# Last head of the forgetting attention: row maxima issued over another stretch, two gate projections moved, buffers re-placed

## The chip, the cores and the metric

The kernel runs on one core of a Trainium2 chip. The core has a matrix engine (PE, with its weight loads listed apart as PEld), a vector engine (DVE), a scalar engine (ACT), a general engine (POOL) and a queue engine (SP) that only starts transfers. Each engine works through its own list of instructions in order and waits at semaphores for the others. The metric is the device time of one execution in microseconds (us), lower is better.

## What is computed

One decoder layer on a sequence of 2048 rows with 1024 columns. The input is normalised and projected; eight heads of forgetting attention (branch A) and eight heads of windowed attention (branch B) work on the projections; each branch's output is multiplied by a gate, both go through one output projection, which is normalised and added to the input. Cut to what matters:

```python
h = rms_norm(x, g_pre[l]) * (1.0 + scale[:, None, :]) + shift[:, None, :]
proj = h @ w_in[l]
qa, ka, va, fa, za, qb, kb, vb, zb = jnp.split(proj, split_points, axis=-1)
oa = forgetting_attention(qa, ka, va, fa + b_fgate[l])   # 8 heads of 64, causal
oa = oa * jax.nn.silu(za)
ob = sliding_window_sink_attention(qb, kb, vb, sinks[l]) # after rope
ob = ob * jax.nn.silu(zb)
y = jnp.concatenate([oa, ob], axis=-1) @ w_out[l]
x = x + gate[:, None, :] * rms_norm(y, g_post[l])
# in forgetting_attention, per block of 128 queries:
s = q @ k.T * d**-0.5 + cum[query] - cum[key]; s = where(causal, s, -inf)
p = softmax(s); out = p @ v
```

## The kernel before

All matrix products are made from pairs of 16-bit numbers (a high and a low part), three matmuls for one product. The kernel has four stages: the start and branch B (to about 454 us of the trace), the heads of branch A (454 to 1017 us), and the output projection, whose first part lies inside the last head of branch A and whose rest runs to the end.

**Heads and steps.** Branch A is 8 heads of 20 steps, 160 steps `s` in all, with `hd, r = divmod(s, 20)`; step 7.3 below means head 7, step 3 (s = 143). A step is one column group of 512 queries (`ci` 0 to 3, in steps 0-1, 2-5, 6-11, 12-19 of a head) against two blocks of 128 keys. Its width `w` is 1024 columns, less in the two steps on the diagonal (896 and 384). A step does: `exp32` (ACT, L1312, from the score tile `sta` to `p`), `high` (ACT, L1320) and, a step later, `low` (DVE, L1323), which split `p` in two 16-bit parts `pha`; the scores of the next step (PE, L1307 and L1308, four matmuls); and the products with the values of the step two back (`pv`, PE, L1333 to L1336). There is one score tile, so the scores of step s+1 wait for `exp32` of step s.

**Work put between.** Two lists are spread over the steps, and they go on PE between `pv` and the next scores:

- `punits`: projection units, each 3 matmuls of 512 columns (L328); 8 units fill one bank, which is then read by ACT and DVE. From step 0.0 on there are 352 of them: for each head 1 to 7 four column groups of query and key (`qk`, written to the tile `T` of that head by `evac_qk`), and for each head 0 to 7 two gate groups (`za`, through `evac_z`: tanh on ACT L378, product on DVE L368, store to `z_d` by POOL L376). A loop near L1057 writes their order: for a head `qk` 0, 1, 2, `za`, `qk` 3, `za`, where the `za` belong to the head before.
- `munits`: the row maxima of the scores (`max_units`): a matmul of up to 512 columns (PE, L1258), then a maximum along the row (DVE, L1261, or L1263 with the mask), and after the last of a group a short chain on DVE (L1270 to L1278) and a small matmul (`ext_rows`, L1216) whose result goes into `T` by a transfer (L1222). They must be done before the head's scores of that group, and run most of a head ahead; 44 of them belong to one head.

How many of each go into a step is set by two running goals. Units: the share of the width `w` done so far, of the width of heads 0 to 6, times 352, plus 14, but no more than 352. Maxima: 26 plus 44/20 for each step, to the end of the list. The two are interleaved, half of them before the next scores and half behind the `pv`.

**The last head.** In step 7.0 `open_out` releases the normalised input h^T (`hT`, four tiles of 16 KB per partition) and puts the output weights `wohl` and buffers there. The 16 pieces of w_out are loaded by SP (L1393) into six buffers of `stpo`, and split by ACT and DVE (`w_out_split`, L1398 and L1399) from step 7.2 on. In steps 7.4 and 7.6 `Out.load` fetches the first two output tiles (the attention output `o_d`, L1413, and the gate `z_d`, L1415), and in 7.6 and 7.8 `Out.turn` transposes them on PE (L1421), multiplies by the gate on DVE (L1430), takes squares on ACT (L1434, into a junk tile), sums them on PE (L1438) and writes the high part on ACT (L1444) and the low part on DVE (L1445), each some ticks after the other. Two ticks make a step. Products of the output projection (`Out.product`, PE L1458) come from step 7.10 on; the rest follows after the last step. The x rows and the y rows of a tile lie in the pool `oxy`.

Of the kernel before, what the change touches and what calls it, by code (L numbers as in the profile page):

```python
# [10 lines left out]
F32 = mybir.dt.float32  # L11
F16 = mybir.dt.float16
# [28 lines left out]
def hybrid_layer(  # L41
# [72 lines left out]


    right = ExitStack()
    hpx = ExitStack()
    hpool = hpx.enter_context(tc.tile_pool(name="hpool", bufs=1))
    wpool = right.enter_context(tc.tile_pool(name="wpool", bufs=2, side="right"))
# [9 lines left out]
    swx = ExitStack()  # L129
    swc = swx.enter_context(tc.tile_pool(name="swc", bufs=1))  # L130

    hT = [hpool.tile([P, 2, KT, CH], F16, name=f"hT{i}") for i in range(NCH)]
# [54 lines left out]
    def after(n, f):  # L187
        late.append([n, f])
# [173 lines left out]

    def evac_z(kt, key, ci):
        def evac(ps, free):
            t = op_.tile([P, CH], F32, tag="tz", name="tz")

            def mul():
                V.scalar_tensor_tensor(t[:], t[:], 1.0, ps, op0=ALU.add, op1=ALU.mult)  # L368
                free()
                if lag[0]:  # L370
                    after(lag[0], store)
                else:
                    store()

            def store():
                G.dma_start(z_d[kt, :, ci * CH:(ci + 1) * CH], t[:])  # L376

            after(1, lambda: A.activation(t[:], ps, AF.Tanh, scale=czs[key][:]))  # L378
            after(2, mul)

        return evac


    xt, rstd, xlate = {}, {}, {}

    def load_x(t):
        if t // 4 == 1:
# [668 lines left out]
    N_V3 = len(punits)  # L1056
    for hd in range(1, 9):  # L1057
        for part in range(6):
            if part in (3, 5):
                add(f"za{(hd - 1) // 2}", za_units(hd - 1, (part - 3) // 2))  # L1060
            elif hd < 8:
                add(f"qk{hd}", qk_units(hd, (0, 1, 2, 0, 3)[part]))
    windows = [Pair(j, i) for j in range(4) for i in range(0, NB, 2)]
    pos = [0]

# [293 lines left out]
            munits += us[:2] + ([ext] if ext else []) + us[2:]  # L1359
            ext = ext2  # L1360
    munits += [lambda: None, lambda: None, ext]
    M_HEAD, M_LEAD, PV_LAG = 44, 26, 2

# [3 lines left out]
    def w_slot(n):  # L1367
        return oio["w"][:, n // KT, n % KT, :]

    def open_out():  # L1370
        nonlocal op_, stp
        foxl.close()
        hpx.close()
        wo = foxo.enter_context(tc.tile_pool(name="wo", bufs=1, reuse_waits="tile"))
        op_ = foxo.enter_context(tc.tile_pool(name="opo", bufs=2, reuse_waits="tile"))
        stp = foxo.enter_context(tc.tile_pool(name="stpo", bufs=6, reuse_waits="tile"))
        oxy = foxo.enter_context(tc.tile_pool(name="oxy", bufs=2, reuse_waits="tile"))
        oio["x"] = lambda: oxy.tile([P, D], F32, tag="xr", name="xr")
        oio["y"] = lambda: oxy.tile([P, D], F32, tag="yg", name="yg")
# [9 lines left out]

    def w_out_load(m):  # L1390
        k, cc = m % KT, slice((m // KT) * CH, (m // KT + 1) * CH)
        w_raw[m] = stp.tile([P, CH], F32, tag="st", name=f"wo{m}")
        SP.dma_start(w_raw[m][:], w_out0[k * P:(k + 1) * P, cc])  # L1393

    def w_out_split(m):
        k, cc = m % KT, slice((m // KT) * CH, (m // KT + 1) * CH)
        raw, hi = w_raw.pop(m), w_slot(k)[:, cc]
        A.activation(hi, raw[:], AF.Copy, scale=wsc[:, k:k + 1])  # L1398
        V.scalar_tensor_tensor(w_slot(8 + k)[:, cc], raw[:], wsc[:, k:k + 1], hi, op0=ALU.mult, op1=ALU.subtract)  # L1399

    oio = {}

    class Out:

# [12 lines left out]
        def turn(self, lag):  # L1417

            px = [bk[bank()][:].rearrange("p (k n) -> p k n", k=4) for _ in range(2)]
            for k in range(KT):  # L1420
                PE.transpose(px[k // 4][:, k % 4, :], self.o[:, k * P:(k + 1) * P], ident[:])  # L1421
            self.hl = wpool.tile([P, 2, KT, P], F16, tag=("whl", "wraw")[self.t % 2], name="oz")
            self.sc = sm(1, "w_pw")
            hi, lo = self.hl[:, 0], self.hl[:, 1]
            gs = sm(1, "w_mx")

            def gate():
                for h in range(2):
                    z = self.z[:, 4 * h:4 * h + 4, :]
                    V.tensor_tensor(z, px[h], z, op=ALU.mult)  # L1430

            def squares_():
                junk = stp.tile([P, KT, P], BF16, tag="st", name="zj")
                A.activation(junk[:], self.z, AF.Square, accum_out=gs[:])  # L1434
# [9 lines left out]
            after(lag + 1, lambda: A.activation(hi, self.z, AF.Copy, scale=self.sc[:]))  # L1444
            after(lag + 2, lambda: V.scalar_tensor_tensor(lo, self.z, self.sc[:], hi, op0=ALU.mult, op1=ALU.subtract))  # L1445

        def product(self, n, k):
            cc = slice(n * CH, (n + 1) * CH)
            if k == 0:
                self.b = bank(True)  # L1450
                if n == 0:
                    self.ss = sm(2, "y_ss")
                else:
                    self.x = oio["x"]()
                    SP.dma_start(self.x[:], xs[self.t * P:(self.t + 1) * P, :])
            py, b = bk[self.b][:], self.b
            for m_, (i, j) in enumerate(((0, 0), (0, 1), (1, 0))):
                PE.matmul(py, self.hl[:, i, k, :], w_slot(8 * j + k)[:, cc],  # L1458
                          start=(k == 0 and m_ == 0), stop=(k == KT - 1 and m_ == 2))
            if k < KT - 1:  # L1460
                return

            def evac():
                if n == 0:
                    self.y = oio["y"]()
                junk = stp.tile([P, 2, CH], BF16, tag="st", name="yj")
                A.activation(junk[:, 0, :], py, AF.Square, accum_out=self.ss[:, n:n + 1])
# [52 lines left out]
    with tc.manual_schedule():  # L1520
# [18 lines left out]
        for _ in range(3):  # L1539
            tick()  # L1540
        steps[0].scores()
        p0, p_tot = pos[0], len(punits) - pos[0]

        w_at = {2: [0], 3: [1], 4: [2], 5: [3], 6: [4], 8: [5], 10: [6], 11: [7], 12: [8], 13: [9], 14: [10],
                15: [11, 12], 16: [13, 14], 17: [15]}
# [109 lines left out]
```

## Time and profile before

| what | value |
|---|---|
| median of 3 runs | 1188.02 us (1186.71 to 1188.46) |
| the profiled execution's own time | 1186.6 us |
| its span, first to last instruction | 1184.9 us |
| mean granted TensorE clock | 0.988 |
| instructions | 27012 |
| step 0.0 begins (first `exp32`) | 453.6 us |
| `exp32` of step 6.7 / 6.16 / 7.0 begins | 902.7 / 933.9 / 943.7 us |
| `exp32` of step 7.4 / 7.10 begins | 953.4 / 976.5 us |

A row of the windows view gives, for a stretch of the span, the busy time of each engine with its number of instructions, the granted TensorE clock as a share of full speed, and the load of the transfer engines. A row of the waits view names an instruction and the one that ended its wait, with the sum, the number of times and the longest. A row of the timeline view has the start, the duration and the instruction. In a timeline, a matmul's duration overlaps the next one, so the time that one takes from PE is the distance between two starts.

### The profile page before, as it was taken

To read this page: it belongs to the slowest core of one execution; us is meant where nothing else is said; L and a number is where in the kernel's file an instruction comes from. 1 tells how busy PE (TensorE), PEld (TensorE's weight loads), DVE (VectorE), ACT (ScalarE), POOL (GpSimd) and SP (SyncE) were. 2 spreads that over 40 slices of the span, in tenths; PEclk is the share of its full clock that TensorE was granted. 3 is DMA by queue.
4 is the path that set the end of the run, shared out by engine and by line. 5 is a ranking of instruction groups with operands and counts; after the bars stand their busy time and mean duration, and the time that the engine had idled before them with its cause. 6 is when DMAs were issued, how large, how long until landed. Compare 5 with 4: busy or idle time off the path is not lost. (4 is left out here: it accounts for less than half of the span.)

```text
span 1184.9 us, 27012 instructions
## 1 busy us (share of the span) xinstructions
PE 1122.8 (95%) x10490; PEld 655.1 (55%) x10490; DVE 919.1 (78%) x2329; ACT 677.6 (57%) x1122; POOL 165.9 (14%) x302
## 2 busy tenths in 40 slices
PE   5899998999989999999999999999999979999996
PEld 1466556644459855555555555555555545555553
DVE  6776577888787657889888897888878897767665
ACT  4676445565456434666766666666766788333331
POOL 1001122233232201211111111011000100000000
PEclk9999999999999999999999999999999989999999
DMA  9645336587667722333323323133121154465652
GB/s 331 213 137 158 94 88 123 113 150 143 141 132 119 130 63 70 78 93 78 85 68 103 75 61 86 45 90 64 40 48 46 59 156 156 147 191 168 210 172 78
DMA packets 162452, 136.36 MB, mean 115 GB/s; under 512 B 95356, under 2 KB 139428, under 8 KB 162324
## 3 DMA queue, kind: packets, MB, share of 16 engines
q1 hardware_dynamic: 152532, 106.65, 35.8%
q0 software_dynamic: 9456, 27.72, 8.9%
q8 instruction: 82, 1.34, 0.5%
q14 instruction: 46, 0.38, 0.1%
q10 hardware_dynamic: 336, 0.26, 0.1%
HBM read 70.97 MB, written 25.18 MB: 81 GB/s over the span
## 5 line engine op out<-in xcount | busy, mean ns | idle before, releaser
L1312 ACT ACTIVATE p<-sta,lift,scl_qk 128x1024 f32<-128x1024 f32 (+2 forms) x160 | 171.7, 1073 | 99.2 <-PE sta L1308 90.7
L328 PE MATMUL bk<-hT,wh_qk 128*128 128x512 f16 x768 | 194.6, 378 | 0.0
L1458 PE MATMUL bk<-wohl,oz 128*128 128x512 f16 x768 | 172.4, 379 | 1.9 <-ACT wohl L1398 0.8
L1323 DVE TENSOR_TENSOR pha<-p,pha 128x1024 f16<-128x1024 f32 (+2 forms) x160 | 169.3, 1058 | 0.2 <-ACT pha L1320 0.2
L1320 ACT ACTIVATE pha<-p 128x1024 f16<-128x1024 f32 (+2 forms) x160 | 148.1, 926 | 35.0 <-POOL p L1316 29.6
L1261 DVE TENSOR_REDUCE a_m<-bk 128x1 f32<-128x512 f32 x192 | 129.8, 684 | 43.6 <-PE bk L1258 43.1
L1458 PEld LDWEIGHTS <-oz 128*128 128x128 f16 x768 | 74.4, 99 | 83.9 <-issue 1.8
L1307 PE MATMUL sta<-T 128*128 128x512 f16 (+1 forms) x320 | 110.7, 351 | 10.5 <-ACT p L1312 10.5
L1333 PE MATMUL poa<-vt,pha 128*128 128x65 f16 x1088 | 117.6, 194 | 2.3 <-DVE ona L1342 2.3
L1336 PE MATMUL poa<-vt,pha 128*128 128x65 f16 x1088 | 117.2, 193 | 1.4 <-DVE pha L1323 1.4
L1335 PE MATMUL poa<-vt,pha 128*128 128x64 f16 x1088 | 117.5, 195 | 0.0
L328 PEld LDWEIGHTS <-wh_qk 128*128 128x128 f16 x768 | 72.4, 97 | 74.7 <-issue 0.6
L1333 PEld LDWEIGHTS <-pha 128*128 128x128 f16 x1088 | 102.4, 97 | 16.8 <-DVE ona L1342 3.2
L1258 PE MATMUL bk<-T 66*128 66x512 f16 (+2 forms) x320 | 109.9, 350 | 1.0 <-DVE a_m L1261 1.0
L1308 PE MATMUL sta<-T 69*128 69x512 f16 (+1 forms) x320 | 109.3, 352 | 0.0
L1335 PEld LDWEIGHTS <-pha 128*128 128x128 f16 x1088 | 101.7, 98 | 13.6 <-issue 0.3
L1336 PEld LDWEIGHTS <-pha 128*128 128x128 f16 x1088 | 101.5, 99 | 1.6 <-DVE pha L1323 1.6
L328 PE MATMUL bk<-hT,wh_za 128*128 128x512 f16 x384 | 99.8, 378 | 0.0
L346 PE MATMUL bk<-wh_va,hT 128*128 128x128 f16 x1536 | 94.3, 221 | 1.7 <-DVE wh_va L272 1.7
L328 PE MATMUL bk<-hT,wh_zb 128*128 128x512 f16 x384 | 92.7, 384 | 2.2 <-DVE wh_zb L272 2.2
L346 PEld LDWEIGHTS <-hT 128*128 128x128 f16 x1536 | 89.0, 99 | 8.3 <-issue 5.9
L1316 POOL TENSOR_SCALAR_AFFINE_SELECT p<-p 128x256 f32<-128x256 f32 x64 | 33.0, 515 | 420.6 <-ACT p L1312 417.9
(487 smaller groups left out, 1860.5 us busy)
## 6 DMA issues: line engine op xcount, KB each, us to landing
wa<-in_w_ada_dram SPq DMA_DIRECT2D x16, 512.0 KB
z_d<-tz POOLq DMA_DIRECT2D x32, 256.0 KB, 3.0
T<-stq SPq DMA_DIRECT2D x128, 64.0 KB
T<-o_d SPq DMA_DIRECT2D x16, 512.0 KB
T<-z_d SPq DMA_DIRECT2D x16, 512.0 KB
xr<-in_x_dram SPq DMA_DIRECT2D x16, 512.0 KB
out_dram<-yg SPq DMA_DIRECT2D x15, 512.0 KB
xt<-in_x_dram SPq DMA_DIRECT2D x12, 512.0 KB
```

The costliest lines, as they stand in the source:

```text
L328: PE.matmul(ps, whl[:, a, k, :], hT[ci][:, b, k, :], start=(k == 0 and n == 0), stop=(k == KT - 1 and n == 2))
L346: PE.matmul(ps[:, u * P:(u + 1) * P], hT[ci][:, a, k, u * P:(u + 1) * P], whl[:, b, k, :], start=(k == 0 and n == 0), stop=(k == KT - 1 an ...
L1258: PE.matmul(mx[:, :w], T[0:XM, 0, i * P:(i + 1) * P], T[0:XM, 2, pc * CH:pc * CH + w], start=True, stop=True)
L1261: V.tensor_reduce(m3[:, u, pc:pc + 1], mx[:, :w], axis=AX.X, op=ALU.max)
L1307: PE.matmul(self.st[:, o:o + w], T[:, 3, kb_], T[:, 1, qc], start=True, stop=False)
L1312: A.activation(self.p32[:, :self.w], self.st[:, :self.w], AF.Exp, scale=scl[f"qk{self.hd}"][:], bias=lift[:])
L1320: A.activation(self.ph[:, 0, :self.w], self.p32[:, :self.w], AF.Copy)
L1323: V.tensor_tensor(self.ph[:, 1, :self.w], self.p32[:, :self.w], self.ph[:, 0, :self.w], op=ALU.subtract)
L1333: PE.matmul(po[:, u, :], ph[:, 0, pq], vt[:, b, hd, 0:65], start=(self.first and n == 0 and u == 0), stop=False)
L1335: PE.matmul(po[:, u, 0:64], ph[:, 0, pq], vt[:, b, hd, 65:VW], start=False, stop=False)
L1336: PE.matmul(po[:, u, :], ph[:, 1, pq], vt[:, b, hd, 0:65], start=False, stop=(self.last and n == len(self.blocks) - 1))
L1458: PE.matmul(py, self.hl[:, i, k, :], w_slot(8 * j + k)[:, cc], start=(k == 0 and m_ == 0), stop=(k == KT - 1 and m_ == 2))
```

## The change

1. **Row maxima.** From step 6.7 on (`m_from` = 127) the goal of the maxima is a line from where they stand to the end of the list, reached with step 7.3 (`m_done` = 143). Before, the list ended with step 7.8.
2. **Projection units.** `P_LAST` = 16 units, the two gate groups of head 7, are held back and issued in steps 7.0 to 7.7, two a step. The others are spread over heads 0 to 6 with 14 ahead, as 322 units for their whole width (before 352, with the cap at the end). By the two goals, units issued in steps 0.0 to 6.6 go from 331 to 304, in 6.7 to 6.15 from 21 to 23, in 6.16 to 6.19 from 0 to 9, in 7.0 to 7.7 from 0 to 16. Maxima go, in the same stretches, from 279 to 279, 20 to 25, 9 to 12, and 18 to 12, and two in step 7.8 to none.
3. **Order.** For head 7, `qk` 3 comes before both `za`.
4. **Places.** The gate units of head 7 read `hT` 2 and 3, so these two tiles now stay (pool `hpb`). The x and y rows of the output tiles lie in `hT[3]`, the w_out pieces from the sixth on and the junk of the squares in `hT[2]`, the last gates in the freed `gw`. `stpo` has 4 buffers in place of 6.

The core of the diff:

```diff
+    hpb = ctx.enter_context(tc.tile_pool(name="hpb", bufs=1))
...
+    hT = [(hpool if i < 2 else hpb).tile([P, 2, KT, CH], F16, name=f"hT{i}") for i in range(NCH)]
...
-            t = op_.tile([P, CH], F32, tag="tz", name="tz")
+            t = oio["z"][ci % 2] if "w" in oio else op_.tile([P, CH], F32, tag="tz", name="tz")[:]
...
-            if part in (3, 5):
-                add(f"za{(hd - 1) // 2}", za_units(hd - 1, (part - 3) // 2))
+            if part in ((4, 5) if hd == 7 else (3, 5)):
+                add(f"za{(hd - 1) // 2}", za_units(hd - 1, part // 5))
             elif hd < 8:
-                add(f"qk{hd}", qk_units(hd, (0, 1, 2, 0, 3)[part]))
+                add(f"qk{hd}", qk_units(hd, ((0, 1, 2, 3) if hd == 7 else (0, 1, 2, 0, 3))[part]))
...
-    M_HEAD, M_LEAD, PV_LAG = 44, 26, 2
+    M_HEAD, M_LEAD, PV_LAG, P_LEAD, P_LAST = 44, 26, 2, 14, 16
...
-        stp = foxo.enter_context(tc.tile_pool(name="stpo", bufs=6, reuse_waits="tile"))
-        oxy = foxo.enter_context(tc.tile_pool(name="oxy", bufs=2, reuse_waits="tile"))
+        stp = foxo.enter_context(tc.tile_pool(name="stpo", bufs=4, reuse_waits="tile"))
+        oxy = [hT[3][:, a, 4 * b:4 * b + 4, :].rearrange("p k n -> p (k n)").bitcast(F32)
+               for a in range(2) for b in range(2)]
...
+        gz = gat.tile([P, D], F32, tag="gw", name="gz")
+        oio["z"] = [gz[:, n * CH:(n + 1) * CH] for n in range(2)]
+        spare = hT[2][:].rearrange("p a k n -> p (a k n)")
+        oio["r"] = [spare[:, 2 * CH * n:2 * CH * (n + 1)].bitcast(F32) for n in range(6)]
+        oio["j"] = [spare[:, CH * a:CH * b].bitcast(BF16) for a, b in ((12, 14), (14, 15), (15, 16))]
...
-        w_raw[m] = stp.tile([P, CH], F32, tag="st", name=f"wo{m}")
+        w_raw[m] = oio["r"][(m - 5) % 6] if m > 4 else stp.tile([P, CH], F32, tag="st", name=f"wo{m}")[:]
...
-        p0, p_tot = pos[0], len(punits) - pos[0]
+        p0, p_tot = pos[0], len(punits) - pos[0] - P_LEAD - P_LAST
+        m_ramp, m_from, m_done = 0, 6 * NS + 7, 7 * NS + 3
...
-            npn = p0 + min(p_tot, 14 + p_tot * w_acc // w_all) - pos[0]
+            npn = p0 + P_LEAD + p_tot * w_acc // w_all - pos[0]
             fil = fill
+            if hd == 7:
+                npn = len(punits) - P_LAST + P_LAST * min(r + 1, 8) // 8 - pos[0]
             if hd == 7 and r >= 8:
                 npn, fil = N_IN * max(r - 9, 0) // (NS - 10) - opos[0], ofill
-            m_goal = min(len(munits), M_LEAD + int(round((s + 1) * M_HEAD / NS)))
+            m_goal = M_LEAD + int(round((s + 1) * M_HEAD / NS))
+            if s == m_from:
+                m_ramp = mi
+            if s >= m_from:
+                m_goal = m_ramp + (len(munits) - m_ramp) * (s + 1 - m_from) // (m_done + 1 - m_from)
+            m_goal = min(len(munits), m_goal)
```

Three places in the engines' lists. The first is PE at the end of head 6, behind the scores of step 6.18 and the `pv` of step 6.15; before, two row maxima stand there and then the next scores:

```order
L1336 LDWEIGHTS pha
L1336 MATMUL poa<-vt,pha 128x65
L1258 LDWEIGHTS T_6391
L1258 MATMUL bk_137<-T_6391 128x512
L1258 LDWEIGHTS T_6391
L1258 MATMUL bk_136<-T_6391 128x384
L1307 LDWEIGHTS T_6390
```

In the change (its lines are numbered a little higher: 329 for 328, 1259 for 1258, 1308 for 1307), the same place begins with:

```order
L1337 LDWEIGHTS pha
L1337 MATMUL poa<-vt,pha 128x65
L1259 LDWEIGHTS T_6394
L1259 MATMUL bk_139<-T_6394 128x512
L329 LDWEIGHTS wh_za_12913
L329 MATMUL bk_6365<-hT_108,wh_za_12913 128x512
L329 LDWEIGHTS wh_za_12913
L329 MATMUL bk_6365<-hT_108,wh_za_12913 128x512
L329 LDWEIGHTS wh_za_12913
L329 MATMUL bk_6365<-hT_108,wh_za_12913 128x512
L1259 LDWEIGHTS T_6394
L1259 MATMUL bk_138<-T_6394 128x512
```

A gate unit of head 6 (three matmuls with the weights `wh_za`) now stands between the maxima of head 7; another unit and a third maximum follow before the next scores.

The second place is PE in the last head, between the `pv` of step 7.2 and the scores of step 7.6 (whose first row ends the piece), before:

```order
L1258 LDWEIGHTS T_6391
L1258 MATMUL bk_137<-T_6391 128x512
L1258 LDWEIGHTS T_6391
L1258 MATMUL bk_136<-T_6391 128x512
L1307 LDWEIGHTS T_6390
```

In the change there stands, ahead of the same scores:

```order
L329 LDWEIGHTS wh_za_12913
L329 MATMUL bk_140<-hT_110,wh_za_12913 128x512
L329 LDWEIGHTS wh_za_12913
L329 MATMUL bk_140<-hT_110,wh_za_12913 128x512
L329 LDWEIGHTS wh_za_12913
L329 MATMUL bk_140<-hT_110,wh_za_12913 128x512
L329 LDWEIGHTS wh_za_12913
L329 MATMUL bk_140<-hT_110,wh_za_12913 128x512
L329 LDWEIGHTS wh_za_12913
L329 MATMUL bk_140<-hT_110,wh_za_12913 128x512
L329 LDWEIGHTS wh_za_12913
L329 MATMUL bk_140<-hT_110,wh_za_12913 128x512
```

Two maxima are gone there, and two gate units of head 7 stand in their place, which read `hT[3]`.

The third place is DVE in the last head, around the first output tile's product with the gate (L1430 before, L1445 in the change). Before, from the `low` of step 7.4 to that of step 7.6:

```order
L1323 TENSOR_TENSOR pha<-p_14169,pha 128x896
L1399 SCALAR_TENSOR_TENSOR wohl<-wo_14095,wsc,wohl 128x512
L1261 TENSOR_REDUCE a_m<-bk_136 128x1
L1263 ISA bk_6362,a_m<-bk_6362,cmask 128x384
L1263 ISA a_m 128x1
L1323 TENSOR_TENSOR pha<-p_14215,pha 128x384
L1399 SCALAR_TENSOR_TENSOR wohl<-wo_14137,wsc,wohl 128x512
L1261 TENSOR_REDUCE a_m<-bk_135 128x1
L1261 TENSOR_REDUCE a_m<-bk_6361 128x1
L1430 TENSOR_TENSOR T_6390<-bk_137,T_6390 128x512
L1430 TENSOR_TENSOR T_6390<-bk_136,T_6390 128x512
L1323 TENSOR_TENSOR pha<-p_14256,pha 128x1024
```

and in the change:

```order
L1324 TENSOR_TENSOR pha<-p_14162,pha 128x896
L1416 SCALAR_TENSOR_TENSOR wohl<-wo_14071,wsc,wohl 128x512
L1324 TENSOR_TENSOR pha<-p_14213,pha 128x384
L1416 SCALAR_TENSOR_TENSOR wohl<-wo_14126,wsc,wohl 128x512
L1445 TENSOR_TENSOR T_6393<-bk_138,T_6393 128x512
L1445 TENSOR_TENSOR T_6393<-bk_6364,T_6393 128x512
L1324 TENSOR_TENSOR pha<-p_14256,pha 128x1024
```

The row maxima (`a_m`, five rows) no longer stand ahead of the gate product.

More of the change, by code (lines that the diff above doesn't have):

```diff
@@ L130, in hybrid_layer @@
     swc = swx.enter_context(tc.tile_pool(name="swc", bufs=1))
-    hT = [hpool.tile([P, 2, KT, CH], F16, name=f"hT{i}") for i in range(NCH)]
+    hT = [(hpool if i < 2 else hpb).tile([P, 2, KT, CH], F16, name=f"hT{i}") for i in range(NCH)]
     cosT = swc.tile([P, S], F32, name="cosT")
@@ L364, in evac @@
         def evac(ps, free):
-            t = op_.tile([P, CH], F32, tag="tz", name="tz")
+            t = oio["z"][ci % 2] if "w" in oio else op_.tile([P, CH], F32, tag="tz", name="tz")[:]
             def mul():
-                V.scalar_tensor_tensor(t[:], t[:], 1.0, ps, op0=ALU.add, op1=ALU.mult)
+                V.scalar_tensor_tensor(t, t, 1.0, ps, op0=ALU.add, op1=ALU.mult)
                 free()
@@ L375, in store @@
             def store():
-                G.dma_start(z_d[kt, :, ci * CH:(ci + 1) * CH], t[:])
-            after(1, lambda: A.activation(t[:], ps, AF.Tanh, scale=czs[key][:]))
+                G.dma_start(z_d[kt, :, ci * CH:(ci + 1) * CH], t)
+            after(1, lambda: A.activation(t, ps, AF.Tanh, scale=czs[key][:]))
             after(2, mul)
         return evac
-    xt, rstd, xlate = {}, {}, {}
+    xt, rstd, xlate, oio = {}, {}, {}, {}
     def load_x(t):
@@ L1375, in open_out, with rotate, next_ @@
         op_ = foxo.enter_context(tc.tile_pool(name="opo", bufs=2, reuse_waits="tile"))
-        stp = foxo.enter_context(tc.tile_pool(name="stpo", bufs=6, reuse_waits="tile"))
-        oxy = foxo.enter_context(tc.tile_pool(name="oxy", bufs=2, reuse_waits="tile"))
-        oio["x"] = lambda: oxy.tile([P, D], F32, tag="xr", name="xr")
-        oio["y"] = lambda: oxy.tile([P, D], F32, tag="yg", name="yg")
+        stp = foxo.enter_context(tc.tile_pool(name="stpo", bufs=4, reuse_waits="tile"))
+        oxy = [hT[3][:, a, 4 * b:4 * b + 4, :].rearrange("p k n -> p (k n)").bitcast(F32)
+               for a in range(2) for b in range(2)]
+        def rotate(key, views):
+            n = [0]
+            def next_():
+                n[0] += 1
+                return views[n[0] % 2]
+            oio[key] = next_
+        gz = gat.tile([P, D], F32, tag="gw", name="gz")
[3 more added lines that the diff above has]
+        oio["j"] = [spare[:, CH * a:CH * b].bitcast(BF16) for a, b in ((12, 14), (14, 15), (15, 16))]
+        rotate("x", oxy[:2])
+        rotate("y", oxy[2:])
         oio["w"] = wo.tile([P, 2, KT, D], F16, name="wohl")
@@ L1391, in w_out_load @@
         k, cc = m % KT, slice((m // KT) * CH, (m // KT + 1) * CH)
-        w_raw[m] = stp.tile([P, CH], F32, tag="st", name=f"wo{m}")
-        SP.dma_start(w_raw[m][:], w_out0[k * P:(k + 1) * P, cc])
+        w_raw[m] = oio["r"][(m - 5) % 6] if m > 4 else stp.tile([P, CH], F32, tag="st", name=f"wo{m}")[:]
+        SP.dma_start(w_raw[m], w_out0[k * P:(k + 1) * P, cc])
     def w_out_split(m):
@@ L1397, in w_out_split @@
         raw, hi = w_raw.pop(m), w_slot(k)[:, cc]
-        A.activation(hi, raw[:], AF.Copy, scale=wsc[:, k:k + 1])
-        V.scalar_tensor_tensor(w_slot(8 + k)[:, cc], raw[:], wsc[:, k:k + 1], hi, op0=ALU.mult, op1=ALU.subtract)
-    oio = {}
+        A.activation(hi, raw, AF.Copy, scale=wsc[:, k:k + 1])
+        V.scalar_tensor_tensor(w_slot(8 + k)[:, cc], raw, wsc[:, k:k + 1], hi, op0=ALU.mult, op1=ALU.subtract)
     class Out:
@@ L1432, in squares_ @@
             def squares_():
-                junk = stp.tile([P, KT, P], BF16, tag="st", name="zj")
-                A.activation(junk[:], self.z, AF.Square, accum_out=gs[:])
+                A.activation(oio["j"][0].rearrange("p (k n) -> p k n", k=KT), self.z, AF.Square, accum_out=gs[:])
             def scale_():
@@ L1465, in evac @@
                     self.y = oio["y"]()
-                junk = stp.tile([P, 2, CH], BF16, tag="st", name="yj")
-                A.activation(junk[:, 0, :], py, AF.Square, accum_out=self.ss[:, n:n + 1])
+                A.activation(oio["j"][1 + n], py, AF.Square, accum_out=self.ss[:, n:n + 1])
                 V.tensor_tensor(self.y[:, cc], py, gacc[:, cc], op=ALU.mult)
```

## Prediction

> **What bounds the kernel now.** I read the page first, for the busy shares and the slices of 29.6 us.
>
> ```profile
> PE 1122.8 (95%) x10490; PEld 655.1 (55%) x10490; DVE 919.1 (78%) x2329; ACT 677.6 (57%) x1122; POOL 165.9 (14%) x302
> PE   5899998999989999999999999999999979999996
> DVE  6776577888787657889888897888878897767665
> ```
>
> PE is busy nearly everywhere, with one low slice (a 7) in the place where the last head begins; there DVE shows 8 and 9. So I cut the span at steps with the windows view (columns: busy of PE, PEld, DVE, ACT, POOL, then granted clock, transfer share, GB/s).
>
> ```profile
> 453.60:902.70 449.10, 443.90 (x4321) 247.06 (x4320) 377.87 (x837) 301.76 (x399) 62.02 (x108) 1.00 0.30 74
> 902.70:933.90 31.20, 31.20 (x318) 17.46 (x315) 23.48 (x53) 21.61 (x27) 1.90 (x4) 1.00 0.12 33
> 933.90:943.70 9.80, 7.92 (x119) 5.19 (x116) 8.85 (x20) 7.59 (x10) 1.35 (x3) 1.00 0.31 109
> 943.70:953.40 9.70, 8.09 (x109) 4.74 (x106) 9.43 (x26) 8.43 (x12) 1.01 (x2) 1.00 0.18 46
> 953.40:976.50 23.10, 17.29 (x178) 11.80 (x177) 21.24 (x41) 17.68 (x23) 1.08 (x2) 0.78 0.55 168
> 976.50:1017.10 40.60, 37.31 (x402) 21.87 (x399) 29.41 (x53) 30.82 (x44) 3.46 (x4) 1.00 0.39 122
> ```
>
> In heads 0 to 6 up to step 6.15 PE is the limit: idle 5.2 of 480 us. From step 6.16 to 7.9 (933.9 to 976.5, 42.6 us) PE is busy 33.3 us and idle 9.3, while DVE is busy 39.5. There the units have run out, and the maxima of head 7 and the splits of w_out make DVE the busiest. The clock falls there too:
>
> ```profile
> 952.00:958.40 6.40, 3.45 (x48) 2.21 (x47) 6.37 (x14) 5.65 (x8) 1.08 (x2) 1.00 0.40 109
> 958.40:961.80 3.40, 3.40 (x31) 2.13 (x30) 3.40 (x6) 2.04 (x4) 0.00 (x0) 0.50 0.48 155
> 968.60:975.50 6.90, 6.33 (x42) 4.56 (x42) 5.30 (x15) 5.58 (x8) 0.00 (x0) 0.51 0.37 109
> ```
>
> In two stretches the granted clock is half. Their PE busy times, 3.40 and 6.33, would be about half at full clock: another 4.8 us lost. So PE loses 9.3 + 4.8 = **14.1 us** between steps 6.16 and 7.9. The waits view of 933 to 977 says for whom:
>
> ```profile
> PE sta L1307 <- ACT p L1312: 5.3, 5, 2.8
> PE poa L1333 <- DVE ona L1342: 2.3, 2, 1.9
> ACT zj L1434 <- DVE T L1430: 2.3, 2, 1.8
> PE bk L1173 <- DVE w_mx L1171: 0.9, 1, 0.9
> PE bk L1216 <- DVE lq L1278: 0.7, 1, 0.7
> ```
>
> PE waits for `exp32`; ACT, in its turn, stands before the squares of the first output tile until DVE has multiplied it with the gate, behind a queue of maxima. The other half of the PE waits names DVE directly.
>
> **The change, part by part.** What a unit and a maximum take from PE is read from the distance of starts in the timeline:
>
> ```profile
> 930.61 0.19 PE L1333 MATMUL poa<-vt,pha 128*128 128x65 f16 x1
> ...
> 931.35 0.81 PE L328 MATMUL bk<-hT,wh_za 128*128 128x512 f16 x3
> 932.00 0.38 PE L1258 MATMUL bk<-T 66*128 66x512 f16 x1
> 932.31 0.22 PE L1216 MATMUL bk<-identh,lq 128*8 128x128 f16 x1
> 932.46 0.39 PE L1307 MATMUL sta<-T 128*128 128x512 f16 x1
> 932.68 0.38 PE L1308 MATMUL sta<-T 69*128 69x512 f16 x1
> ```
>
> A unit: 932.00 - 931.35 = 0.65 us. A matmul of 512 columns: 932.68 - 932.46 = 0.22, which I take for a maximum too. A full `pv`: 931.35 - 930.61 = 0.74.
>
> *Spread of units.* 27 units leave steps 0.0 to 6.6, where PE idles 5.2 of 449 us: 27 x 0.65 = **17.6 us earlier**. What hides nothing must be checked: DVE keeps its 377.87 us in what would be 431.5, 88%, ACT 70%. PE stays the fullest.
>
> *What arrives.* Steps 6.7 to 6.15 get 2 units and 5 maxima, 2 x 0.65 + 5 x 0.22 = 2.4 us, in a stretch with no idle PE: all on the path. Steps 6.16 to 7.9 get 25 units and lose some 5 maxima net: 16.3 - 1.1 = 15.2 us of PE work. These sum to zero against the 17.6, as they must: no work is added, so **the gain is what PE stops losing**, 14.1 us at most in this stretch.
>
> *What PE still loses there.* The wait at L1173 (0.9) is a sum of squares in step 6.16 that the change leaves where it is: kept. Of the 0.7 at L1216 I keep 0.3, since a unit now stands between. The waits for `ona` (2.3) go: no maxima stand ahead of it on DVE from 7.3 on. The largest rest is in steps 7.7 to 7.9, which get one unit and where ACT is full. Its rows of before:
>
> ```profile
> 966.88 1.06 ACT L1434 ACTIVATE zj<-T 128x1024 bf16<-128x1024 f32 x1 [1.76 <-DVE T L1430]
> 967.84 0.19 ACT L1434 ACTIVATION_READ_ACCUMULATOR zj<-T 128x1 f32 x1
> 967.94 1.19 ACT L1312 ACTIVATE p<-sta,lift,scl_qk 128x1024 f32<-128x1024 f32 x1
> 969.02 0.71 ACT L1398 ACTIVATE wohl<-wo,wsc 128x512 f16<-128x512 f32 x1
> 969.64 1.04 ACT L1320 ACTIVATE pha<-p 128x1024 f16<-128x1024 f32 x1
> 971.07 1.21 ACT L1312 ACTIVATE p<-sta,lift,scl_qk 128x1024 f32<-128x1024 f32 x1 [0.40 <-PE sta L1308]
> 972.67 1.15 ACT L1444 ACTIVATE oz<-T,w_pw 128x1024 f16<-128x1024 f32 x1 [0.40 <-DVE w_pw L113]
> L378 ACT ACTIVATE tz<-bk,cz_za 128x512 f32<-128x512 f32 x4 | 2.7, 682 | 0.8 <-PE bk L328 0.8
> L1421 PE MATMUL bk<-ident,T 128*128 128x128 f32 x48 | 7.2, 300 | 0.1
> ```
>
> In the change ACT has there three `exp32` (3.6), three `high` (3.1), two squares with their read (2.5), the split of a piece (0.7), the high part of the tile (1.15) and a gate's tanh (0.7, new): 11.7, less 0.1 of overlap for each of 11 (967.94 to 969.02 is 1.08 for a duration of 1.19): 10.6 us. PE has three sets of scores (2.6), `pv` (two full, one small, 1.8), one unit (0.65) and a set of transposes (8 x 0.15 = 1.2): about 6.5. So it still loses 10.6 - 6.5 = 4.1 us. Left over: 0.9 + 0.3 + 4.1 = 5.3, and 14.1 - 5.3 = **8.8 us gained**. At half clock nothing is left in this sum.
>
> *Clock, row against rule.* Before the first slow stretch PE was busy 3.45 of 6.40 us, in waits of at most 2.8 us. The Trainium skill, page "TensorE: Matmul & The Clock Gate", section "HAM oscillation", says that PE idle gaps longer than about 3.4 us bring the slow clock. By that rule no gap of before was long enough, so the trace disagrees: many shorter ones did it. By the row the slow clock may return behind steps 7.7 to 7.9, where PE is busy 6.5 of 10.6 us: 3.2 us more (half of 6.33), which I keep for the range.
>
> *Weights of the next head.* The high part of the next head's weights overwrites a buffer that PE still reads:
>
> ```profile
> ACT wh_qk L266 <- PE bk L328: 10.7, 6, 2.8
> PE sta L1307 <- ACT p L1312: 5.2, 5, 1.9
> ```
>
> (Waits of 453 to 902 us.) Six times ACT waits for PE, and behind it PE for `exp32`, 5.2 us in all. The slower spread shifts each of the six against its step. Where it stands in front of a step's `high`, PE has the next scores and `pv` to cover it; where it stands behind, it delays the next `exp32`. The change has one of six behind, before two. I take 1.5 us off; the bounds are all 5.2 gone, and every one like the longest, 6 x 1.9 = 11.4, so 6.2 more.
>
> *Buffers and the queue.* A piece of w_out in `hT[2]` waits for gate units that end in step 7.3, and is split in 7.8 or later. The fourth piece, still in `stpo`, now waits on SP for a gate store of head 6 in the same place:
>
> ```profile
> z_d<-tz POOLq DMA_DIRECT2D x32, 256.0 KB, 3.0
> L368 DVE SCALAR_TENSOR_TENSOR tz<-tz,bk 128x512 f32<-128x512 f32 x4 | 2.7, 678 | 0.0
> ```
>
> POOL can start that store in step 7.1, and the first row (DMA issues, median time to landing last) has such a store landing after 3.0 us. Behind it on SP stand a store of `o_d`, a row transfer and the loads of the first output tiles, due in 7.4. I cost it at nothing; should the store land after 7.4, each us delays the gate product by one. `qk` 3 of head 7 ends in 6.13 and its maxima begin in 6.17, four steps that cover the transfer. Two gate products on DVE (0.68 each, the second row) and two tanh on ACT (0.68) in the last head lie beside PE, but for the one tanh counted above.
>
> Sum: -8.8 - 1.5 = **-10.3 us**. The profiled execution took 1186.6, so 1176.3; the median of the runs lies 1.4 above it, so I forecast 1177.7.
>
> **Rivals.**
>
> 1. *PE does not set the pace of heads 0 to 6; DVE does.* Then the units leave a hole and nothing comes earlier, while the 17.6 us still arrive: 1177.7 + 17.6 = 1195.3, slower. It decides from a returned share of 7.3 of 17.6, 41%, downwards, or where DVE's 377.87 us in 453.6 to 902.7 were to meet a PE below it. Against: PE idles 1% there and DVE 16%. For: DVE would stand at 88%, in clumps of weight splits. The Trainium skill, "Perfetto Trace Analysis", section "Identifying the Most-Contended Engine", judges PE not by matmul time but by weight loads (here 55%), and by that rule DVE (78%) comes first, which is this rival; the idle rows of DVE speak against it here.
> 2. *The last head keeps its chain.* The first output tile's loads, not the maxima, hold the gate product, and ACT stays late; the slow clock returns. Then only the waits of 6.16 to 7.3 go: of 14.1 us those up to 953.4 are 1.9 + 1.6 = 3.5 and some of the 2.3 for `ona`, about 5 in all, 1183.
> 3. *The change does not do what it says.* A late transfer of the query and key of head 7, or the SP wait above, puts a new wait of the size of the old ones on PE: 1187 to 1190, no change.
>
> **How the numbers follow.** Forecast (1173 to 1180.7) 0.58; rival 2 (1180.7 to 1185) 0.18; better than 1173, with the weight waits all gone too, 0.08; no change 0.07; slower, by rival 1 in part or whole, 0.09. A change of 0.2% (2.4 us) is about what a measurement of this kernel can tell. The range 1171.0 to 1185.5 takes the slow clock (+3.2), most of the weight waits (-3.7 to +7.7) and rival 2, and leaves out no change and slower.
>
> **What would show it.** Right: between 453.6 us and step 6.7 the span is 16 to 19 us shorter with PE idle about as before; steps 6.16 to 7.9 take some 49 us (42.6 + 15.2 - 8.8) with PE busy over 85%; no half clock before 7.7; the wait of PE for `ona` gone. Wrong: more DVE-released PE waits in heads 1 to 5 (rival 1); ACT's wait for L1430's successor as long as before, released by a transfer (rival 2); PE waits at the maxima of head 7 released by transfers into `T` (rival 3).

## The result and the profile after

| what | before | after |
|---|---|---|
| median, run side by side | 1187.66 us (1186.71 to 1188.46, 4 runs) | 1179.11 us (1177.03 to 1180.07, 4 runs) |
| ratio to before | 1 | 0.9926, 95% interval 0.9914 to 0.9938 |
| the profiled execution's own time | 1186.6 us | 1180.07 us |
| its span | 1184.9 us | 1178.3 us |
| step 0.0 begins | 453.6 us | 455.4 us |
| from step 0.0 to the end of the span | 731.3 us | 722.9 us |

The change makes the kernel 0.6 to 0.9% faster. The forecast was 1177.7, so 1.4 us too low.

The start and branch B were not changed, but the profiled execution of after happens to be 1.8 us longer there (the last section shows where). So the last line of the table, -8.4 us, is the fair difference of the two profiles, and it agrees with the -8.55 of the medians.

The windows view of after, cut at the same steps as the rows of before in the prediction: steps 0.0 to 6.6, 6.7 to 6.15, 6.16 to 6.19, 7.0 to 7.3, 7.4 to 7.9, 7.10 to 7.19 with what follows 7.19 at once, and the rest (columns: busy of PE, PEld, DVE, ACT, POOL, granted clock, transfer share, GB/s).

```profile
455.40:888.60 433.20, 427.47 (x4237) 238.98 (x4236) 374.95 (x834) 300.25 (x394) 61.08 (x107) 1.00 0.29 73
888.60:921.00 32.40, 32.40 (x318) 17.82 (x315) 26.16 (x60) 21.55 (x26) 1.41 (x2) 1.00 0.21 46
921.00:936.30 15.30, 14.43 (x160) 8.29 (x157) 11.95 (x26) 8.71 (x11) 1.38 (x3) 1.00 0.05 18
936.30:948.60 12.30, 12.30 (x129) 7.04 (x126) 11.00 (x28) 9.31 (x11) 1.36 (x3) 1.00 0.45 135
948.60:971.00 22.40, 17.64 (x207) 10.99 (x203) 17.35 (x28) 18.41 (x25) 1.78 (x3) 1.00 0.67 202
971.00:1010.50 39.50, 36.73 (x395) 21.78 (x396) 28.16 (x51) 30.74 (x43) 2.98 (x5) 1.00 0.37 119
1010.50:1178.30 167.80, 158.42 (x802) 80.17 (x800) 110.94 (x337) 49.06 (x95) 0.00 (x0) 0.98 0.53 170
```

Row by row against before: -15.9 (449.10 to 433.20), +1.2 (31.20 to 32.40), +7.4 in the three rows of steps 6.16 to 7.9 (42.60 to 50.00), -1.1 (40.60 to 39.50), and nothing in the rest. That is -8.4. PE is busy 44.37 of the 50.0 us between 6.16 and 7.9, 89%, at full clock throughout. It idles 5.6 us there, where before it lost 9.3 to idling and 4.8 to the half clock.

The waits of PE in heads 0 to 6 of after (455 to 889 us), with the wait of ACT for the next head's weights:

```profile
PE sta L1308 <- ACT p L1313: 3.3, 4, 1.4
PE bk L1259 <- DVE a_m L1262: 1.1, 1, 1.1
PE poa L1334 <- DVE ona L1343: 0.7, 2, 0.4
PE bk L329 <- DVE a_m L1262: 0.6, 2, 0.4
ACT wh_qk L267 <- PE bk L329: 9.1, 6, 2.8
```

Before, there was only the first kind of PE's waits, 5.2 us of it, and ACT's wait was 10.7. Now three kinds of waits for DVE, 2.4 us in all, stand beside 3.3. They fit a PE that, with fewer units between its other work, reaches the row maxima and the values sooner than DVE has done its part.

Of the waits of after in steps 6.16 to 7.9 (920 to 972 us), those on the way to PE's idle time, and the first two transfers that SP issues from 953 us on (start, duration, queue, line, transfer):

```profile
DVE T L1445 <- DMA T<-z_d: 3.8, 1, 3.8
PE sta L1308 <- ACT p L1313: 3.0, 2, 2.6
ACT hT L1448 <- DVE T L1445: 2.6, 1, 2.6
PE poa L1334 <- DVE ona L1343: 0.9, 1, 0.9
PE bk L1174 <- DVE w_mx L1172: 0.9, 1, 0.9
```

```profile
953.69 0.33 SPq L1428 DMA_DIRECT2D T<-o_d  x1
954.07 0.42 SPq L1430 DMA_DIRECT2D T<-z_d  x1
```

The chain of before is still there. The gate product of the first output tile (L1445) waits for its gate from memory, ACT's squares (L1448) wait for that product, the next `exp32` stands behind the squares, and PE waits for `exp32`. PE's longest wait for `exp32` is nearly as long (2.6 us against 2.8), the sum of these waits is smaller (3.0 against 5.3). It is a transfer that holds the gate product, not the row maxima. And so it was before, as DVE's timeline of before shows:

```profile
965.56 1.29 DVE L1430 TENSOR_TENSOR T<-bk,T 128x512 f32<-128x512 f32 x2 [0.23 <-DMA T<-z_d]
```

The row maxima stood ahead of the product in the list, but DVE was done with them 0.2 us before the gate arrived. With the gate's load issued at the same time, the product could not have started earlier without them.

### The profile page after: what moved, and what is told of

It reads as the page before. It is cut to its first block, busy times and chain, and to the rows that moved or that the text cites. A ratio compares the mean times of both kernels' runs of the same rounds, so it can differ in the third digit from the quotient of the medians.

```text
span 1178.3 us, 26992 instructions
## 1 busy us (share of the span) xinstructions
PE 1119.8 (95%) x10490; PEld 653.0 (55%) x10490; DVE 918.9 (78%) x2329; ACT 679.1 (58%) x1122; POOL 165.3 (14%) x302
## 5 line engine op out<-in xcount | busy, mean ns | idle before, releaser
L329 PE MATMUL bk<-hT,wh_qk 128*128 128x512 f16 x768 | 197.9, 378 | 0.6 <-DVE a_m L1262 0.6
L1336 PEld LDWEIGHTS <-pha 128*128 128x128 f16 x1088 | 101.0, 97 | 13.4
```

Source lines behind the costliest of these rows:

```text
L329: PE.matmul(ps, whl[:, a, k, :], hT[ci][:, b, k, :], start=(k == 0 and n == 0), stop=(k == KT - 1 and n == 2))
L1336: PE.matmul(po[:, u, 0:64], ph[:, 0, pq], vt[:, b, hd, 65:VW], start=False, stop=False)
```

## Experiments

All times are medians; each ratio is to the kernel before, run beside it. The last column is the profile's span from step 0.0 on (before 731.3, after 722.9), which leaves the unchanged start out.

| kernel | median us | ratio, 95% interval | from step 0.0, us |
|---|---|---|---|
| row maxima alone | 1191.7 | 1.0039, 1.0025 to 1.0054 | 735.8 |
| units alone | 1178.63 | 0.9930, 0.9913 to 0.9946 | 722.4 |
| no units held for head 7 | 1189.9 | 1.0017, 1.0007 to 1.0028 | 730.8 |
| places alone | 1186.7 | 0.9995, 0.9986 to 1.0004 | 730.5 |
| gate loaded early | 1178.85 | 0.9935, 0.9921 to 0.9949 | 723.0 |
| held units over ten steps | 1177.3 | 0.9920, 0.9908 to 0.9933 | 722.3 |
| weights later | 1174.66 | 0.9901, 0.9886 to 0.9917 | 720.5 |
| these three, old maxima | 1171.84 | 0.9877, 0.9864 to 0.9891 | 715.9 |
| before, weights later | 1181.52 | 0.9956, 0.9942 to 0.9971 | 725.2 |
| the three less early gate | 1172.16 | 0.9881, 0.9865 to 0.9898 | 715.9 |

### Row maxima alone

The kernel before, with the new goal of the maxima and nothing else:

```diff
+        m_ramp, m_from, m_done = 0, 6 * NS + 7, 7 * NS + 3
...
-            m_goal = min(len(munits), M_LEAD + int(round((s + 1) * M_HEAD / NS)))
+            m_goal = M_LEAD + int(round((s + 1) * M_HEAD / NS))
+            if s == m_from:
+                m_ramp = mi
+            if s >= m_from:
+                m_goal = m_ramp + (len(munits) - m_ramp) * (s + 1 - m_from) // (m_done + 1 - m_from)
+            m_goal = min(len(munits), m_goal)
```

> The kernel before with only the row maxima of the last head issued by step 7.3; units and places as before. Filling theory (the gain is what PE stops losing between steps 6.16 and 7.9, and needs both parts): DVE is freed in 7.4 to 7.8 but PE has no units there and DVE gets fuller in 6.16 to 7.3; 3 to 4 us gained, about 1184. Rival A, the maxima are the change: 1179 to 1181. Rival B, the maxima bring nothing without units: 1187 to 1188.

It is slower, by 0.25 to 0.54%, which none of the expectations had. Its windows of steps 6.7 to 6.15 and 6.16 to 7.9, and the three largest sums of waits that PE has there:

```profile
904.90:937.00 32.10, 32.10 (x325) 18.11 (x323) 25.50 (x59) 21.79 (x27) 1.91 (x4) 1.00 0.11 32
937.00:981.70 44.70, 32.80 (x395) 21.49 (x391) 37.74 (x78) 33.90 (x42) 4.05 (x7) 0.85 0.43 133
```

```profile
PE sta L1307 <- ACT p L1312: 3.9, 3, 3.4
PE bk L1216 <- DVE lq L1278: 3.1, 2, 2.1
PE poa L1333 <- DVE ona L1342: 3.0, 2, 1.7
```

Before, these two stretches took 31.2 and 42.6 us, so 3.0 us are lost here. The waits at L1216 grew from 0.7 to 3.1 us and those for `ona` from 2.3 to 3.0. This fits maxima that fill DVE's queue earlier (it is busy 25.50 us in the first stretch, 23.48 before), so that PE waits for DVE sooner; that link is argued, not shown. Of the profile's 4.5 us, the other 1.5 lie in heads 0 to 6, where this profile has a half-clock stretch that before has not (last section).

### Units alone

The changed kernel, with the old goal of the maxima:

```diff
-            m_goal = M_LEAD + int(round((s + 1) * M_HEAD / NS))
-            if s == m_from:
-                m_ramp = mi
...
+            m_goal = min(len(munits), M_LEAD + int(round((s + 1) * M_HEAD / NS)))
```

> The changed kernel with the row maxima as before (to step 7.8); units spread and held back as changed. Filling theory: PE is filled, but DVE keeps the maxima and the first output tile's product stays behind them; 4 to 6 us gained, 1182 to 1184, and PE still waits for DVE in 7.4 to 7.8. Rival A, maxima are the change: 1186 to 1188. Rival B, the units are all of it: 1179 to 1180.

The whole gain is there without the maxima. The windows of its steps 6.16 to 6.19, 7.0 to 7.3, 7.4 to 7.7 and 7.8 to 7.9:

```profile
919.70:934.20 14.50, 13.55 (x155) 8.01 (x152) 10.03 (x19) 8.32 (x9) 1.37 (x3) 1.00 0.05 19
934.20:946.40 12.20, 12.20 (x130) 6.88 (x127) 10.65 (x27) 9.50 (x12) 1.36 (x3) 1.00 0.43 142
946.40:959.80 13.40, 13.40 (x145) 8.15 (x142) 13.37 (x25) 10.88 (x14) 1.61 (x3) 1.00 0.66 204
959.80:967.70 7.90, 5.90 (x76) 3.92 (x72) 7.69 (x19) 7.57 (x12) 0.00 (x0) 1.00 0.42 126
```

DVE is full in 7.4 to 7.7 (13.37 of 13.4 us) with the maxima back in its queue, and PE is busy all of those 13.4 us. So the place of the maxima is not what decides there: with units to do, PE is busy beside a full DVE. The stage is 2.0 us shorter than in after (48.0 against 50.0), but steps 7.10 to 7.19 take 41.9 in place of 39.5, so the two kernels end alike.

### No units held for the last head

```diff
-    M_HEAD, M_LEAD, PV_LAG, P_LEAD, P_LAST = 44, 26, 2, 14, 16
+    M_HEAD, M_LEAD, PV_LAG, P_LEAD, P_LAST = 44, 26, 2, 14, 0
```

> The changed kernel with no unit held back for head 7 (the slower spread then ends with head 6; the last 16 units lie in heads 0 to 6); maxima as changed. Filling theory: 6.16 to 6.19 are filled, 7.0 to 7.7 have PE idle again; gain between 4 and 6, 1182 to 1184. Rival, that the held units do not matter: 1179 to 1180. Rival, that they are all of it: 1186 to 1188.

The gain is gone; the time lies above what any of the expectations had, and nearest to the one that the held units are all of it. Its windows of steps 0.0 to 6.6, 6.7 to 6.15 and 6.16 to 7.9:

```profile
454.10:895.50 441.40, 436.04 (x4283) 243.53 (x4282) 375.38 (x835) 299.01 (x396) 63.76 (x107) 1.00 0.30 74
895.50:927.90 32.40, 32.40 (x317) 18.07 (x314) 26.24 (x60) 21.67 (x26) 1.91 (x4) 1.00 0.14 38
927.90:976.10 48.20, 39.03 (x433) 24.62 (x430) 38.08 (x76) 35.25 (x43) 4.21 (x8) 0.89 0.41 129
```

Two moves of units can be told apart here. Those that leave steps 0.0 to 6.6 for the end of head 6 (12 by the two goals) give 7.7 us (449.1 to 441.4) and take 1.2 + 5.6 back: they are paid nearly in full, as PE idles only 1.9 us in steps 6.16 to 6.19 of before (and the new goal of the maxima is in this sum too). The 16 of the last head are paid only in small part. With them, heads 0 to 6 lose 8.2 us more (441.4 to 433.2) while the stage of 6.16 to 7.9 grows by only 1.8 (48.2 to 50.0). PE's idle time falls there from 9.2 to 5.6 us and its clock rises from 0.89 to 1.00.

The profiled execution, 1186.6 us, is the shortest of this kernel's ten; most took about 1190. What adds some 3 us in the others no trace shows.

### Places alone

The changed kernel's buffers, with the order and the goals of before for units and maxima (of the diff in front, the lines on `hpb`, `hT`, `oio`, `stpo` and `oxy` stay):

```diff
-            npn = p0 + P_LEAD + p_tot * w_acc // w_all - pos[0]
+            npn = p0 + min(p_tot, P_LEAD + p_tot * w_acc // w_all) - pos[0]
...
-            if hd == 7:
-                npn = len(punits) - P_LAST + P_LAST * min(r + 1, 8) // 8 - pos[0]
```

> The changed kernel's places of buffers with the units and maxima of before. All theories: the same as before within 1.5 us, 1186.2 to 1189.2, and the first stage as long as before within 1 us; if places matter, 2 us or more to one side.

No difference: 0.9995, with an interval that takes in 1. Six buffers of `stpo` made four, and the pieces in h^T's place, cost nothing by themselves.

### Gate loaded early

```diff
+            if hd == 7 and r in (1, 3):
+                outs[r // 2].load_z()
             if hd == 7 and r in (4, 6):
                 outs[r // 2 - 2].load()
```

Here `load_z` is the gate's half of `Out.load`, which `load` then leaves out for these two tiles.

> The changed kernel, with the z loads of the first two output tiles issued in steps 7.1 and 7.3 in place of 7.4 and 7.6 (the o loads stay). Theory 'the load is the next link': in the changed kernel the gate product stands 3.8 us for its z load and PE loses 2.7 us in 7.4 to 7.7; with the wait gone the time falls by 2 to 3 us against the changed kernel, to 1176 to 1177. Rival 'beside the path': the run with the old maxima has no such wait on DVE and 2.8 us less of lost PE time in 7.4 to 7.7, and yet takes the same 1178.6, because 7.8 to 7.11 lose 2.3 us more; then the time stays within 0.8 us of the changed kernel.

The time stays: 1178.85. The waits of steps 6.16 to 7.9 say why:

```profile
DVE T L1450 <- DMA T<-o_d: 3.9, 1, 3.9
ACT hT L1453 <- DVE T L1450: 2.7, 1, 2.7
PE bk L1441 <- DMA T<-o_d: 1.7, 1, 1.7
```

The gate product (L1450 here) waits as long as in after, now for the attention output of its tile, which is still loaded in step 7.4. That load has itself become slower. In after, PE transposes the tile at 958.8 us, 5.1 us after the issue of its load, without a wait that the profile shows. Here PE waits 1.7 us for it, until 959.8, 6.9 us after the issue at 952.9. What slows it no run shows; the second tile's gate load, issued just ahead of it at 951.3, is one candidate.

### Held units over ten steps

```diff
-                npn = len(punits) - P_LAST + P_LAST * min(r + 1, 8) // 8 - pos[0]
-            if hd == 7 and r >= 8:
+                npn = len(punits) - P_LAST + P_LAST * min(r + 1, 10) // 10 - pos[0]
+            if hd == 7 and r >= 10:
```

> The changed kernel, with its 16 held units spread over ten steps, 7.0 to 7.9, in place of eight. Theory 'room in 7.8 and 7.9': PE has 4.9 us of work in 7.4 us there, so three units (2.0 us) fit into its gaps and come out of full steps ahead: 1 to 2 us faster than the changed kernel, 1177 to 1178. Rival 'ScalarE is the bound there': it is busy 7.4 of 7.4 us in these two steps, and each unit brings it a tanh; then the two steps grow by what the eight ahead of them lose, and the time is the changed kernel's, or up to 1 us above.

Its median is 1.8 us under after's, but the intervals of the two ratios lie mostly on each other, and by the profiles only 0.6 us (722.3 against 722.9) is gained. The windows of steps 7.0 to 7.7 and 7.8 to 7.9:

```profile
933.30:959.70 26.40, 24.44 (x253) 14.29 (x250) 21.79 (x45) 20.16 (x27) 3.40 (x6) 0.94 0.54 168
959.70:966.50 6.80, 6.03 (x76) 4.16 (x74) 5.21 (x11) 6.80 (x10) 0.00 (x0) 1.00 0.81 261
```

In 7.8 to 7.9 PE idles 0.8 us, in after 2.5 (of 7.4), though ACT is busy all the time: the room is there. But the eight steps ahead now lack units, and a stretch of half clock is back in them (0.94).

### Weights later

The q/k weights' high part is made 7 units before they are used instead of 9, the first half of the low part 5 instead of 6 (the scale, which the expectation names too, stays at 14):

```diff
             leads = (46, 36, 26, 15, 11, 8, 7, 5) if key[:2] in ("va", "zb") else (46, 36, 26, 14, 9, 6, 4, 3)
+            if key[:2] == "qk":
+                leads = (46, 36, 26, 14, 7, 5, 4, 3)
```

> The changed kernel, with the scale, the high and the low parts of the q/k weights made up to two units later, so that ScalarE's high part finds the units that free its place done. Theory 'the wait is the loss': PE's waits for the exponentials behind these high parts, 3.3 us in heads 0 to 6, go in part: 1.5 to 3 us faster than the changed kernel, 1176 to 1177.5. Rival 'the wait moves': ScalarE's copies stand ahead of exponentials at another place, or the units wait for weights that come late; between no change and 3 us slower.

Faster, 1174.66, and by more than the expectation had. Its window of heads 0 to 6 up to step 6.6:

```profile
455.60:884.80 429.20, 426.75 (x4240) 239.12 (x4239) 374.42 (x833) 300.64 (x395) 60.95 (x107) 1.00 0.30 74
```

4.0 us less than after's 433.20: PE idles 2.5 us in place of 5.7. ACT's wait for PE at the weights (9.1 us in after) and PE's for `exp32` (3.3) are gone from the list; the three kinds of waits for DVE stay as they were. In this one profile 1.6 us come back later: steps 7.10 to 7.19 take 1.0 more, and 6.16 to 7.9 take 0.6 more.

### The three together, with the old maxima

> The changed kernel with the three edits together (z loads in 7.1 and 7.3, held units over ten steps, weights two units later) and with the maxima's old goal. If each edit takes away a loss of its own, some 4 to 6 us under the changed kernel, 1173 to 1175; if each only moves a wait, 1178 to 1180; if the late weights make units wait, above 1180.

1171.84 us, the shortest time here and under the 1173 to 1175 that was expected: 0.9877 of before. Its windows of steps 0.0 to 6.6, 6.7 to 6.15, and 6.16 to 7.9:

```profile
455.10:884.30 429.20, 426.75 (x4239) 239.09 (x4238) 374.52 (x833) 300.62 (x395) 60.94 (x107) 1.00 0.30 74
884.30:915.80 31.50, 31.50 (x310) 17.40 (x307) 23.79 (x53) 21.59 (x26) 1.31 (x2) 1.00 0.21 48
915.80:963.50 47.70, 44.82 (x490) 26.81 (x486) 41.71 (x85) 35.61 (x44) 5.13 (x9) 1.00 0.38 120
```

Against after: -4.0 in heads 0 to 6, as with the weights alone, -0.9 in steps 6.7 to 6.15, about as in units alone, and -2.3 in 6.16 to 7.9, where PE idles 2.9 us instead of 5.6.

### Before, with the weights later

The same two lines in the kernel before:

> The kernel before, with nothing but the scale, high and low parts of the q/k weights up to two units later. It sizes the term of the prediction that put the waits for these high parts at 1.5 us. Theory 'the wait is the whole loss': PE's 5.2 us of waits for exponentials in heads 0 to 6 go, as the 3.3 us went in the changed kernel (4.0 us less there), and the time falls by 4 to 6 us, to 1181 to 1183. Rival 'only with fewer units': with 27 more units in heads 0 to 6 ScalarE's copies meet another wait, and less than 2 us go: above 1185.

1181.52 us, 0.29 to 0.58% faster than before. Its window of steps 0.0 to 6.6:

```profile
454.40:897.70 443.30, 443.27 (x4319) 246.94 (x4318) 377.22 (x837) 301.98 (x398) 60.59 (x108) 1.00 0.30 75
```

PE idles 0.03 us where it idled 5.2, and the stretch is 5.8 us shorter. The waits at the weights were a loss of their own that one changed line of numbers takes away, with or without the change of this case.

### The three less the early gate

> The three edits together with the old maxima's goal, less the earlier z loads. The z loads alone gave 0.3 us. If they are worth nothing here either, 1171.5 to 1172.5, the time of the three together; if, with the units over ten steps, the gate product stands for its load again and nothing covers it, 1173.5 to 1175.

1172.16 us, and by the profile 715.9 from step 0.0 on, the same as with the early loads. They are worth nothing here either. The last 7 us come from the other three, the weights, the ten steps and the maxima's old place. The 4.0 us of heads 0 to 6 belong to the weights; the other two these runs do not take apart.

## Why the prediction was right, and where it missed

The forecast of the profiled change was -10.3 us; it is -8.4.

- **Steps 0.0 to 6.6: forecast -17.6, and -1.5 for the weights; measured -15.9.** Right in kind, just under the 16 to 19 us that it named: PE sets the pace of heads 0 to 6. Two terms are off in size. The 27 units take 16.4 us of busy time with them (443.90 to 427.47), 0.61 us each and not 0.65. And PE's idle time did not fall by 1.5 us but rose by 0.5 (5.2 to 5.7): the waits at the weights fell by 1.9, close to the term, but waits for DVE of 2.4, which the sum had at nothing, came in their place. "What hides nothing must be checked" was answered by DVE's mean of 88%; a mean does not say that DVE is late at single points. Units alone has the same rows; with no units held, where 15 more units lie in these steps, the waits for DVE come to 0.2 us. The count behind the 1.5 is not borne out either: one costly place of six was to be left, and PE still waits at four. The bound "all 5.2 gone" is reached when the weights' lead is changed, as the two runs with later weights show.
- **Steps 6.7 to 6.15: forecast +2.4, measured +1.2.** In units alone the maxima stay where they were, and the stretch is 0.8 us shorter than in after.
- **Steps 6.16 to 7.9: forecast 49 us, +6.4; measured 50.0, +7.4.** PE lost 14.1 us before, and 5.3 were to be left; 5.6 are. Of the 8.5 us that PE stopped losing, 4.8 are the half clock and 3.7 idle time. The PE work that came in is 15.9 us (44.37 against 42.6 - 14.1 = 28.5), forecast 15.2. Steps 6.16 to 6.19 keep the 0.9 at the sum of squares, as forecast. For steps 7.7 to 7.9 the forecast was 4.1 us of idle PE:

```profile
957.70:971.00 13.30, 9.46 (x118) 6.35 (x114) 9.00 (x14) 10.69 (x14) 0.00 (x0) 1.00 0.86 269
```

  And two groups of PE in the same stretch:

```profile
L329 PE MATMUL bk<-hT,wh_za 128*128 128x512 f16 x9 | 2.4, 379 | 0.0
L1436 PE MATMUL bk<-ident,T 128*128 128x128 f32 x16 | 2.1, 275 | 0.0
```

  PE idles 3.8 of 13.3 us there, and ACT's work is 10.69 (forecast 10.6). But the stretch is longer than ACT's work by the 2.6 us that ACT stands before the squares, and PE had 9.46 us of work, not 6.5 (the listed terms add up to 6.25). The rows name most of the rest: three units (9 matmuls) and two sets of transposes where the prediction counted one of each. The difference came out right by luck, because both terms were about 3 us too small.
- **The reason given for this stage was half wrong.** The prediction held that the maxima ahead of the gate product keep ACT and so PE waiting, and that their earlier place ends the waits for `ona`. The row of before at 965.56 us already speaks against the first: the product's last wait was for its gate. Maxima alone make the kernel slower, units alone give all of the gain, and with no units held it is gone. What ends PE's loss is work to do during the waits. The waits for `ona` fell from 2.3 to 0.9 us in after, and to nearly nothing (0.3 us) with the maxima back in their old place.
- **Steps 7.10 to 7.19: not in the forecast; measured -1.1.** PE is busy 0.6 us less there and idles 0.5 less (40.60 - 37.31 before, 39.50 - 36.73 after). Without it the two profiles would differ by 7.3 us, so part of the closeness of the sum is luck too.
- **Buffers and SP at nothing: right.** The places alone change no time. The two stores of head 6's gates start at 934.2 and 940.9 us and land after 3.3 us at most, ahead of step 7.4 (948.6).
- **Rival 1 fell:** DVE stands at 87% in steps 0.0 to 6.6 (374.95 of 433.20), and 15.9 of 17.6 us were returned; its sign, PE waits for DVE in these heads, did show, with 2.4 us. **Rival 2 was half true:** the transfer does hold the gate product, for 3.8 us, but the slow clock did not come back and other work covers part of the wait (PE idles 2.6 us at its end). **Rival 3 fell:** no wait of PE from step 0.0 to 7.19 is for a transfer.

## What to carry to other kernels

Work that needs nothing is worth most where the engine that sets the pace waits for others: 16 units moved into such a place cost 1.8 us there and gave 8.2 where they left, while units moved only to the end of head 6, where PE idled little, gave 0.9 net of the 7.7 us that they left. Look first for such room, and only then at the chain that makes the wait: moving one link of it (the maxima, one of two loads) brought nothing here. Before an instruction is blamed for a wait, read which one ended it: the row of the gate product named the transfer, not the maxima. A small wait that repeats in every head is a term of its own, to be measured alone: the waits at the weights, 5.2 us in the profile of before, were worth about 5 us of the median there.

## What the runs showed of the hardware

The half clock does not follow from the length of a wait alone. Ahead of step 0.0, where the two kernels run the same instructions, the waits view has PE wait 2.9 us for a transfer in before and 2.1 us in after, and only the shorter wait has a half-clock stretch behind it. The windows of before and of after:

```profile
349.00:352.80 3.80, 0.95 (x29) 0.85 (x27) 3.68 (x10) 0.00 (x0) 2.48 (x6) 1.00 0.87 178
352.80:356.30 3.50, 3.50 (x66) 3.38 (x65) 3.07 (x9) 1.81 (x5) 1.26 (x3) 1.00 0.35 55
```

```profile
349.00:352.80 3.80, 1.66 (x18) 0.86 (x16) 3.64 (x13) 1.26 (x4) 1.58 (x3) 1.00 0.77 155
352.80:356.30 3.50, 3.50 (x46) 3.50 (x43) 3.21 (x8) 0.52 (x1) 1.83 (x4) 0.51 0.62 113
```

In 3.5 us the fast clock starts 66 matmuls, the slow one 46; this is about the 1.8 us by which after's step 0.0 comes later. The same happens in head 3 behind a wait of 1.9 us in both: at full clock in before, at 0.72 over the next 6 us with the maxima alone.

```profile
701.00:707.00 6.00, 6.00 (x71) 3.65 (x70) 5.51 (x10) 4.46 (x8) 0.40 (x1) 1.00 0.32 71
```

```profile
702.00:708.00 6.00, 6.00 (x61) 3.34 (x60) 4.53 (x8) 3.47 (x7) 0.00 (x0) 0.72 0.37 89
```

The Trainium skill, page "TensorE: Matmul & The Clock Gate", section "HAM oscillation", names idle gaps over about 3.4 us as the cause. These waits are all shorter, so the trace disagrees with that bound; and a stretch that comes in one execution and not in another makes a spread of 1.5 to 1.8 us here that the order of the instructions does not explain. What decides it stays open. Over the last 78 to 97 us up to step 7.10 the granted clock is steadier: 0.93 or 0.94 in the five kernels with no units in the last head, 0.98 to 1.00 in the seven with them.
